# Broadcasting a gain row by products with ones, and multiplying two weight tiles on half the tokens before the other half is normed

## The chip, the cores and the metric

The kernel runs on one core of one Trainium2 chip. The metric is the device time of one execution in microseconds (us). A core has these engines, by the names of the profile: PE (TensorE, matrix products; its weight loads are listed apart as PEld), DVE (VectorE), ACT (ScalarE), POOL (GpSimd) and SP (SyncE, which here issues the DMAs). Each engine works through its own queue of instructions in a fixed order, and waits at an instruction whose semaphores have not come.

## The reference, cut to what matters

The program is one layer of a hybrid encoder on 1024 tokens of width 1024 in fp32: a mixer of windowed attention and a bidirectional gated DeltaNet, then cross attention into 256 memory tokens, then a SwiGLU network.

```
def _rms_norm(x, gain):
    xf = x.astype(jnp.float32)
    y = xf * lax.rsqrt(jnp.mean(xf * xf, axis=-1, keepdims=True) + EPS)
    return (y * gain.astype(jnp.float32)).astype(x.dtype)
...
        h = _rms_norm(x, g_mix_pre[l])
        proj = h @ w_in[l]
        aq, ak, av, dqkv, dgate, dalpha, dbeta = jnp.split(proj, IN_SPLITS, axis=-1)
...
        mix = jnp.concatenate([attn_o, dn_o], axis=-1) @ w_out[l]
        x = x + _rms_norm(mix, g_mix_post[l])
```

The change touches the first two lines of the layer: the input norm, and the first two 128-column tiles of `dqkv` (the first key head and the first query head), which a convolution over five tokens follows.

## The kernel before, in words

Every fp32 operand of a product is split into a high part, rounded by ACT, and a low part, the difference, made by DVE or POOL (`split`, lines 102 and 103). A product of two such operands is three PE products: high with high, low with high, high with low. The tiles are named by it: `hhi` and `hlo` hold the normed input, with tokens on the free axis, and `whi` and `wlo` a weight tile.

The order of the work is not written by hand. The program is written step by step, a scheduler with a timeline simulation puts the instructions of each engine in a static order when the program is built, and a tile pool (a number of buffers under one tag) adds the waits for a free buffer. `tc.high_priority` moves weight loads ahead in that order, and `tc.issue_after(i)` keeps the instructions inside it behind instruction i.

The start works as follows.

- SP loads x in eight tiles of 128 tokens (`xt`, 512 KB each, six buffers, lines 205 and 217), and `gmix` (line 207), the gain row copied to all 128 partitions by the DMA itself: 512 KB written for a row of 4 KB.
- For each tile t, ACT squares it and sums (line 220), POOL makes the reciprocal root `rs` in two small instructions (`rstd_of`, lines 159 and 160), and DVE multiplies the tile with `rs` and `gmix` in place (line 223, the scaling). PE transposes the tile in eight 128x128 pieces into two PSUM banks of the pool `ps` (line 228), ACT casts each bank to `hhi`, and DVE subtracts to give `hlo`.
- Two weight tiles of `w_in` are loaded (`load_w`), rounded on ACT and subtracted on DVE. Then `gemm_b` (line 260) multiplies: tile 1 and tile 0 on tokens 0 to 511, 24 products each, then both on tokens 512 to 1023. The results stay in the PSUM pool `pg` of three banks.
- `conv` (lines 275 to 287) reads each pair of accumulators with ACT (`cp` and `acc`, lines 282 and 283, one of each for each half), then DVE adds four taps (line 285).

In the program's text all eight tiles are normed first, and the products come after. In the static order PE has two products ahead of the last transposes, and the transposes of tiles 6 and 7 between products of the first half.

Between about 400 and 620 us lie the DeltaNet scan, the attention windows (scores `psw`, transposed probabilities `ptw`, outputs `pow`, copied to `ao` and stored to the DRAM tile `d_mix`) and the memory keys and values. The values are `pcv` (line 907); ACT copies them to `vv` (line 911, one buffer) and SP stores them to `d_mv` (line 912). After it the mixer's output product `pmg` (line 994) reads `d_mix` back: `mraw` (line 1033) is split into `b`, and the weights `w_out` are loaded by `load_w`.

Of the kernel before, what the change touches and what calls it, by code (L numbers as in the profile page):

```python
# [10 lines left out]
F32 = mybir.dt.float32  # L11
F32R = mybir.dt.float32r
I32 = mybir.dt.int32
AF = mybir.ActivationFunctionType
ALU = mybir.AluOpType
# [4 lines left out]
P = 128  # L20
S = 1024
D = 1024
KT = D // P
# [3 lines left out]
EPS = 1e-6  # L27
# [48 lines left out]
def tile_hybrid_block(  # L76
# [6 lines left out]
    nc = tc.nc  # L83
    x, mem, out = x[0], mem[0], out[0]
    w_in, w_out, w_cq, w_ckv, w_co = w_in[0], w_out[0], w_cq[0], w_ckv[0], w_co[0]
    w_gate_up, w_down = w_gate_up[0], w_down[0]

    if dump is None:
        def dump(name, ap):
            pass  # L90


    def f32(ap):
        return ap.bitcast(F32)
# [4 lines left out]
    def split(hi, lo, src, scale=None, eng=None):  # L99

        if scale is None:
            nc.scalar.copy(hi, src)  # L102
            (eng or nc.vector).tensor_tensor(lo, src, f32(hi), ALU.subtract)  # L103
        else:
            nc.scalar.activation(hi, src, AF.Identity, scale=scale)
            nc.vector.scalar_tensor_tensor(lo, src, scale, f32(hi), ALU.mult, ALU.subtract)

    def pool(name, bufs, **kw):
        return tc.tile_pool(name=name, bufs=bufs, reuse_waits="tile", **kw)
# [8 lines left out]
    def load_w(src, k, n, eng=None, after=None):  # L118

        with tc.high_priority(AHEAD):  # L120
            raw = wp.tile([P, k, n], F32, tag="wraw", name="wraw")
            with ExitStack() as order_:
                if after:
                    order_.enter_context(tc.issue_after(after.ins))
                nc.sync.dma_start(raw, src.rearrange("(k p) n -> p k n", p=P))
            hi = wp.tile([P, k, n], F32R, tag="whi", name="whi")
            lo = wp.tile([P, k, n], F32R, tag="wlo", name="wlo")
            split(hi, lo, raw, eng=eng)
        return hi, lo
# [26 lines left out]
    def rstd_of(rs, ss, n, eps):  # L156

        w = ss.shape[-1]
        nc.gpsimd.tensor_scalar(rs, ss, n, eps, ALU.mult, ALU.add)
        nc.gpsimd.tensor_tensor(rs, rs, mhalf[:, :w], ALU.pow)  # L160
# [30 lines left out]
    pg = pgs.enter_context(pool("pg", 3, space=PSUM))  # L191
# [3 lines left out]
    t1 = pa1.enter_context(pool("t1a", 2, side="right"))  # L195

    def small():
        return ps.tile([P, 512], F32, tag="ps", name="ps")


    xts = [t1.tile([P, D], F32, tag="xt", name="xt", bufs=6) for _ in range(6)]
    gmix = t1.tile([P, D], F32, tag="gmix", name="gmix", bufs=1)
    xload = []
    for t in range(6):
        xload.append(nc.sync.dma_start(xts[t], x[t * P:(t + 1) * P, :]))
        if t == 0:
            nc.sync.dma_start(gmix, g_mix_pre[0].partition_broadcast(P))
            nc.sync.dma_start(ident, consts[:, 0:P])
    hT = []
    for hf in range(2):  # L210
        hi = hx.tile([P, KT, HALF], F32R, name=f"hhi{hf}")
        lo = hx.tile([P, KT, HALF], F32R, name=f"hlo{hf}")
        for j in range(4):
            t = 4 * hf + j
            xt = xts[t] if t < 6 else t1.tile([P, D], F32, tag="xt", name="xt", bufs=6)
            if t >= 6:
                nc.sync.dma_start(xt, x[t * P:(t + 1) * P, :])
            junk = t1.tile([P, D], F32, tag="junk", name="junk", bufs=1)
            ss = t1.tile([P, 1], F32, tag="ss", name="ss", bufs=4)
            nc.scalar.activation(junk, xt, AF.Square, accum_out=ss)  # L220
            rs = t1.tile([P, 1], F32, tag="rs", name="rs", bufs=4)
            rstd_of(rs, ss, 1.0 / D, EPS)
            nc.vector.scalar_tensor_tensor(xt, xt, rs, gmix, ALU.mult, ALU.mult)
            for kq in range(2):
                pt = small()
                for k in range(4):
                    c = (4 * kq + k) * P
                    nc.tensor.transpose(pt[:, k * P:(k + 1) * P], xt[:, c:c + P], ident)
                o = slice(4 * kq, 4 * kq + 4), slice(j * P, (j + 1) * P)
                split(hi[:, o[0], o[1]], lo[:, o[0], o[1]], pt.rearrange("p (k t) -> p k t", k=4))  # L230
        hT.append((hi, lo))
        dump(f"hT{hf}", (hi, lo))


    rows = early.tile([P, P], F32, name="rows")
    nc.gpsimd.memset(rows, 0.0)
# [4 lines left out]
    pt = small()  # L241
# [13 lines left out]
    def gemm_b(whi, wlo, act, psums, nk=KT):  # L255

        for ah, p_ in zip(act, psums):
            for k in range(nk):
                for i, (w, a) in enumerate(((whi, 0), (whi, 1), (wlo, 0))):
                    nc.tensor.matmul(p_, w[:, k, :], ah[a][:, k, :], start=(k == 0 and i == 0),  # L260
                                     stop=(k == nk - 1 and i == 2))

    def proj(src_cols, eng=None):
# [2 lines left out]
        gemm_b(whi, wlo, hT, pp)  # L266
        return pp

    pa1.close()
    tb = p12.enter_context(pool("tb", 1))  # L270
    pp_ = ExitStack()
# [3 lines left out]
    def conv(pp, ci):  # L275
        cp = tcv.tile([P, S + 4], F32, tag="cp", name="cp", bufs=2)
        nc.gpsimd.memset(cp[:, 0:2], 0.0)
        nc.gpsimd.memset(cp[:, S + 2:S + 4], 0.0)
        acc = tcv.tile([P, S], F32, tag="acc", name="acc", bufs=3)
        taps = [cols[:, t * 12 + ci:t * 12 + ci + 1] for t in range(5)]  # L280
        for hf in range(2):
            nc.scalar.copy(cp[:, 2 + hf * HALF:2 + (hf + 1) * HALF], pp[hf])
            nc.scalar.activation(acc[:, hf * HALF:(hf + 1) * HALF], pp[hf], AF.Identity, scale=taps[2])  # L283
        for t in (0, 1, 3, 4):
            nc.vector.scalar_tensor_tensor(acc, cp[:, t:t + S], taps[t], acc, ALU.mult, ALU.add)  # L285
        nc.scalar.activation(acc, acc, AF.Silu)
        return acc

    def dcols(i, h):
        return w_in[:, 768 + (4 * i + h) * P:768 + (4 * i + h + 1) * P]  # L290


    ws = [load_w(dcols(i, 0), KT, P, after=xload[t]) for i, t in ((1, 1), (0, 3))]
    pps = [[None, None], [None, None]]
    for hf in range(2):
        for i in range(2):
            pps[i][hf] = pg.tile([P, 512], F32, tag="pg", name="pg")
            gemm_b(*ws[i], hT[hf:hf + 1], [pps[i][hf]])
    kqv0 = [conv(pps[0], 4), conv(pps[1], 0)]
    pa1 = ExitStack()  # L300
    t1 = pa1.enter_context(pool("t1b", 1, side="right"))
# [8 lines left out]
    for hf in range(2):  # L310
        pp = pg.tile([P, 512], F32, tag="pg", name="pg")
        for k in range(KT):
            for a in range(2):
                nc.tensor.matmul(pp, wabr[:, k, :], hT[hf][a][:, k, :], start=(k == 0 and a == 0),
                                 stop=(k == KT - 1 and a == 1))
        nc.scalar.copy(abT[:, hf * HALF:(hf + 1) * HALF], pp[0:32, :])
    pt = small()
# [42 lines left out]
    pt = small()  # L360
# [41 lines left out]
    pt = small()  # L402
# [195 lines left out]
    def window(n, g):  # L598
# [54 lines left out]
        for j in range(nb):  # L653
            pp = pw.tile([P, 512], F32, tag="pw", name="ptw")
            for hh in range(4):
                nc.tensor.transpose(pp[:, hh * P:(hh + 1) * P], pr[hh][:, j * P:(j + 1) * P], ident)
            ph = tw.tile([P, 512], F32R, tag="ph", name="ph")
            pl = tw.tile([P, 512], F32R, tag="pl", name="pl")
            split(ph, pl, pp)
            for i, (vv, pe_) in enumerate(((vhi, ph), (vhi, pl), (vlo, ph))):  # L660
                nc.tensor.matmul(po.rearrange("p h t -> p (h t)"), vv[:, j].rearrange("p r e -> p (r e)"), pe_,  # L661
                                 start=(j == 0 and i == 0), stop=(j == nb - 1 and i == 2))
# [19 lines left out]
    def delta_proj(h):  # L682
        kqv[h] = kqv.get(h, [])
        for i in (1, 0, 2)[len(kqv[h]):]:
            kqv[h].append(conv(proj(dcols(i, h), nc.gpsimd), 4 * i + h))
# [251 lines left out]
    pg = p3.enter_context(pool("pg3", 4, space=PSUM, side="right"))  # L937
# [190 lines left out]
    def turned_k(xn, k):  # L1128
        pt = pn.tile([P, 512], F32, tag="pn", name="ptn")
        for j in range(4):  # L1130
            nc.tensor.transpose(pt[:, j * P:(j + 1) * P], xn[j][:, k * P:(k + 1) * P], ident)
        return pt

    for k in range(KT):
        pt = turned_k(xn, k)
# [5 lines left out]
    for k in range(HK):  # L1141
        p0, p1 = turned_k(xn, k), turned_k(xn, k + HK)
        g0, g1 = gain("ffn", k), gain("ffn", k + HK)
        x12, t1, t2_, t3_ = (tr.tile([P, HALF], F32, name=f"r{i}", tag=f"r{i}") for i in range(4))
# [50 lines left out]
    pg = L0.enter_context(pool("pg4", 8, space=PSUM))  # L1195

    def bank(name):
        return pg.tile([P, 512], F32, tag="pg", name=name)
# [3 lines left out]
    ws = LA.enter_context(pool("ws", 2, side="right"))  # L1202
# [92 lines left out]
    pps = [bank("pd") for _ in range(NT)]  # L1295
# [25 lines left out]
    for t in range(NT):  # L1321
# [20 lines left out]
        rs = tp_.tile([P, 1], F32, tag="frs", name="frs")  # L1342
# [38 lines left out]
```

## Time and profile before

| | us |
|---|---|
| three runs | 1642.16, 1633.44, 1635.32 |
| median | 1635.32 |
| the profiled execution | 1637.34 |
| its span in the profile | 1635.6 |
| PE busy | 1554.2 (95%) |
| DVE busy | 942.7 (58%) |
| ACT busy | 750.8 (46%) |
| POOL busy | 548.9 (34%) |

The span runs from the first to the last record of the profile; 1.7 us of the execution lie outside of it. Busy shares are means over stages with different limits: in the first 50 us PE is busy for 36.2, and over the whole span DVE, ACT and POOL have idle time that costs nothing. A line of the timeline gives a start and a duration, the engine, the line of the kernel, the operation, output and inputs with their shapes, and in brackets how long the engine stood before it and what it waited for. PE's matmuls are pipelined: a product whose record is 0.39 us long starts 0.23 us after the one before it.

### The profile page before, as it was taken

How to read it: one execution, taken by the hardware profiler on the slowest of the kernel's cores; microseconds unless marked ns; L12 is line 12 of the kernel's file. 1: busy time of each engine (PE TensorE's matmuls, PEld its weight loads, DVE VectorE, ACT ScalarE, POOL GpSimd, SP SyncE). 2: the span in 40 equal slices, each digit the busy share in tenths (PEclk: the TensorE clock that was granted, in tenths of full speed). 3: DMA queues.
4: the chain of work that ended last, by engine and by line, in shares of the span. 5: the costliest groups of instructions: out<-in, count | busy, mean ns of one | idle time of the engine just before them, and what ended most of it. 6: DMA issues, size and time to landing. Idle time of an engine off the chain costs nothing.

```text
span 1635.6 us, 21442 instructions
## 1 busy us (share of the span) xinstructions
PE 1554.2 (95%) x7690; PEld 1301.3 (80%) x7690; DVE 942.7 (58%) x1431; ACT 750.8 (46%) x1518; POOL 548.9 (34%) x501
## 2 busy tenths in 40 slices
PE   6999889999899978999999999999999999999997
PEld 5878778777799857788888777888888888888886
DVE  6855986966668745443346458776555553334332
ACT  6556552237768764554336565233333232444211
POOL 2467553334337400253202221343333441321100
PEclk9999999898999998999999999999999999999999
DMA  6134257574999593454223164442223223565452
GB/s 201 41 116 130 64 166 208 140 181 133 320 320 289 149 293 112 151 184 146 74 65 116 52 213 151 126 135 77 78 90 96 79 84 114 202 214 183 140 175 73
DMA packets 267815, 240.47 MB, mean 147 GB/s; under 512 B 43176, under 2 KB 216637, under 8 KB 267709
## 3 DMA queue, kind: packets, MB, share of 16 engines
q1 hardware_dynamic: 267709, 239.11, 47.2%
q8 instruction: 60, 0.98, 0.3%
q14 instruction: 46, 0.38, 0.1%
HBM read 177.69 MB, written 58.75 MB: 145 GB/s over the span
## 4 chain that ended last, share of the span: by engine, by line
PE 67%; DVE 9%; DMA 6%; issue 3%; ACT 3%; POOL 2%; SPq 1%; POOLq 0%; ACTq 0%; DVEq 0%
PE pmg L994 10%; PE pd L1335 8%; PE pd L1311 7%; PE pE L1165 7%; PE pD L1165 7%; PE pA L1165 6%; PE pcq L260 5%; PE pB L1165 3%; PE psc L763 3%; PE pcs L1074 1%; PE pg L260 1%; DVE acc L285 1%; PE pco L1100 1%; PE pow L661 1%; DVE tmpb L510 1%
## 5 line engine op out<-in xcount | busy, mean ns | idle before, releaser
L102 ACT CAST whi<-wraw 128x1024 fp32r<-128x1024 f32 x108 | 113.4, 1050 | 167.3 <-issue 60.0
L103 POOL TENSOR_TENSOR wlo<-wraw,whi 128x1024 fp32r<-128x1024 f32 x48 | 118.3, 2464 | 174.4 <-ACT whi L102 156.1
L260 PE MATMUL pg<-hhi,whi 128*128 128x512 f32 x352 | 141.7, 404 | 0.2 <-ACT hhi L102 0.2
L260 PE MATMUL pg<-hlo,whi 128*128 128x512 f32 x352 | 141.5, 402 | 0.0
L260 PE MATMUL pg<-hhi,wlo 128*128 128x512 f32 x352 | 141.4, 402 | 0.0
L994 PE MATMUL pmg<-whi,b 128*128 128x512 f32 x384 | 119.8, 402 | 15.2 <-ACT b L102 12.6
L103 DVE TENSOR_TENSOR wlo<-wraw,whi 128x1024 fp32r<-128x1024 f32 x60 | 74.6, 1245 | 92.6 <-ACT whi L102 88.4
L1165 PE MATMUL pA<-b,whi 128*128 128x512 f32 x352 | 109.5, 392 | 1.4 <-ACT m L1182 1.4
L994 PEld LDWEIGHTS pmg<-whi,b 128*128 128x128 f32 x384 | 73.4, 193 | 32.1 <-ACT b L102 13.4
L285 DVE SCALAR_TENSOR_TENSOR acc<-cp,cols,acc 128x1024 f32<-128x1024 f32 x48 | 75.6, 1576 | 34.3 <-ACT acc L283 33.6
L1242 POOL TENSOR_TENSOR act<-act,up 128x512 f32<-128x512 f32 x33 | 48.4, 1468 | 106.6 <-issue 57.0
L260 PEld LDWEIGHTS pg<-hhi,wlo 128*128 128x128 f32 x352 | 68.0, 193 | 13.6
L260 PEld LDWEIGHTS pg<-hhi,whi 128*128 128x128 f32 x352 | 67.8, 193 | 13.5 <-ACT hhi L102 0.4
L260 PEld LDWEIGHTS pg<-hlo,whi 128*128 128x128 f32 x352 | 67.9, 193 | 13.3
L1165 PEld LDWEIGHTS pA<-b,whi 128*128 128x128 f32 x352 | 65.3, 188 | 15.1 <-ACT m L1182 2.0
L994 PE MATMUL pmg<-wlo,b 128*128 128x512 f32 x192 | 71.3, 392 | 0.0
L1165 PE MATMUL pA<-b,wlo 128*128 128x512 f32 x176 | 68.7, 391 | 1.1 <-DVE wlo L103 1.1
L1335 PE MATMUL pd<-wdh,ath 128*128 128x512 f32 x176 | 69.4, 395 | 0.0
L1335 PE MATMUL pd<-wdh,atl 128*128 128x512 f32 x176 | 69.4, 395 | 0.0
L1335 PE MATMUL pd<-wdl,ath 128*128 128x512 f32 x176 | 69.4, 395 | 0.0
L1311 PE MATMUL pd<-dl,whi 128*128 128x512 f32 x176 | 68.5, 389 | 0.0
L1311 PE MATMUL pd<-dh,wlo 128*128 128x512 f32 x176 | 68.3, 389 | 0.0
(392 smaller groups left out, 4145.0 us busy)
## 6 DMA issues: line engine op xcount, KB each, us to landing
wraw<-in_w_gate_up_dram SPq DMA_DIRECT2D x52, 512.0 KB, 3.9
kv<-d_kv SPq DMA_DIRECT2D x32, 512.0 KB, 7.1
wraw<-in_w_in_dram SPq DMA_DIRECT2D x22, 512.0 KB, 4.2
araw<-d_act SPq DMA_DIRECT2D x22, 512.0 KB, 3.4
draw<-in_w_down_dram SPq DMA_DIRECT2D x22, 512.0 KB, 4.3
atr<-d_act SPq DMA_DIRECT2D x16, 704.0 KB, 4.8
d_act<-act SPq DMA_DIRECT2D x40, 256.0 KB, 2.3
d_kv<-kv SPq DMA_DIRECT2D x8, 1024.0 KB, 6.4
```

The costliest lines, as they stand in the source:

```text
L102: nc.scalar.copy(hi, src)
L103: (eng or nc.vector).tensor_tensor(lo, src, f32(hi), ALU.subtract)
L260: nc.tensor.matmul(p_, w[:, k, :], ah[a][:, k, :], start=(k == 0 and i == 0), stop=(k == nk - 1 and i == 2))
L285: nc.vector.scalar_tensor_tensor(acc, cp[:, t:t + S], taps[t], acc, ALU.mult, ALU.add)
L510: nc.vector.tensor_tensor(tv, A[:, j + 1:, j:j + 1].to_broadcast([P, n, j]), A[:, j:j + 1, 0:j].to_broadcast([P, n, j]), ALU.mult)
L661: nc.tensor.matmul(po.rearrange("p h t -> p (h t)"), vv[:, j].rearrange("p r e -> p (r e)"), pe_, start=(j == 0 and i == 0), stop=(j == nb ...
L763: nc.tensor.matmul(out[:, d, h, :], lt[:, d, h, :], rt[:, d, h, :], start=True, stop=True)
L994: nc.tensor.matmul(pp[t], act[a][:, k, tt], w_[:, kk, :], start=(k == 0 and i == 0), stop=(k == KT - 1 and i == 2))
L1165: nc.tensor.matmul(out_, w[a][:, k, :], xx[b_][:, k, :], start=(start and k == 0 and i == 0), stop=(k == HK - 1 and i == 2), skip_group_ch ...
L1242: nc.gpsimd.tensor_tensor(o_, o_, up, ALU.mult)
L1311: nc.tensor.matmul(pps[t], a[:, tt], b_, start=(f == 0 and i == 0), stop=(f == NF - 1 and i == 2))
L1335: nc.tensor.matmul(pp, a[:, f - f0], b_[:, f], start=(f == 0 and i == 0), stop=(f == NF - 1 and i == 2))
```

## The change

It has three parts.

1. The 512 KB load of `gmix` is replaced by a load of the row alone (`grow`, 1x1024, 4 KB). POOL fills a row of ones (`one`, 1x128), PE makes two products of one row each (ones by 512 gains) into `ps` banks, and ACT copies the banks to `gmix`.
2. The norm becomes `norm_half(hf)`. The loads of the two weight tiles and their products move up in the text: norm of tiles 0 to 3, both weight tiles on tokens 0 to 511, norm of tiles 4 to 7, both weight tiles on tokens 512 to 1023. An order is added: the square, the root and the scaling of tile t stay behind the last `hlo` of tile t-2 (tiles 4 and 5: of tile 3), so that tiles keep their order.
3. The subtraction that gives `wlo` of the second weight tile (column tile 0) goes from DVE to POOL.

```diff
@@ in split @@
-            (eng or nc.vector).tensor_tensor(lo, src, f32(hi), ALU.subtract)
+            return (eng or nc.vector).tensor_tensor(lo, src, f32(hi), ALU.subtract)
@@ the input norm @@
     gmix = t1.tile([P, D], F32, tag="gmix", name="gmix", bufs=1)
+    grow = t1.tile([1, D], F32, tag="grow", name="grow", bufs=1)
+    one = t1.tile([1, P], F32, tag="one", name="one", bufs=1)
+    nc.gpsimd.memset(one, 1.0)
...
         if t == 0:
-            nc.sync.dma_start(gmix, g_mix_pre[0].partition_broadcast(P))
+            nc.sync.dma_start(grow, g_mix_pre)
             nc.sync.dma_start(ident, consts[:, 0:P])
+
+    for c in range(0, D, 512):
+        pt = small()
+        nc.tensor.matmul(pt, one, grow[:, c:c + 512], start=True, stop=True)
+        nc.scalar.copy(gmix[:, c:c + 512], pt)
     hT = []
-    for hf in range(2):
+
+    done = []
+
+    def norm_half(hf):
...
-            nc.scalar.activation(junk, xt, AF.Square, accum_out=ss)
             rs = t1.tile([P, 1], F32, tag="rs", name="rs", bufs=4)
-            rstd_of(rs, ss, 1.0 / D, EPS)
-            nc.vector.scalar_tensor_tensor(xt, xt, rs, gmix, ALU.mult, ALU.mult)
+
+            wait = done[3] if t in (4, 5) else done[t - 2] if t > 1 else None
+            with ExitStack() as order_:
+                if wait:
+                    order_.enter_context(tc.issue_after(wait.ins))
+                nc.scalar.activation(junk, xt, AF.Square, accum_out=ss)
+                rstd_of(rs, ss, 1.0 / D, EPS)
+                nc.vector.scalar_tensor_tensor(xt, xt, rs, gmix, ALU.mult, ALU.mult)
...
-                split(hi[:, o[0], o[1]], lo[:, o[0], o[1]], pt.rearrange("p (k t) -> p k t", k=4))
+                lo_at = split(hi[:, o[0], o[1]], lo[:, o[0], o[1]], pt.rearrange("p (k t) -> p k t", k=4))
+            done.append(lo_at)
...
+    norm_half(0)
...
@@ ahead of the convolutions @@
+    ws = [load_w(dcols(i, 0), KT, P, e, after=xload[t]) for i, t, e in ((1, 1, None), (0, 3, nc.gpsimd))]
+    pps = [[None, None], [None, None]]
+    for hf in range(2):
+        if hf:
+            norm_half(1)
+        for i in range(2):
+            pps[i][hf] = pg.tile([P, 512], F32, tag="pg", name="pg")
+            gemm_b(*ws[i], hT[hf:hf + 1], [pps[i][hf]])
...
-    ws = [load_w(dcols(i, 0), KT, P, after=xload[t]) for i, t in ((1, 1), (0, 3))]
-    pps = [[None, None], [None, None]]
-    for hf in range(2):
-        for i in range(2):
-            pps[i][hf] = pg.tile([P, 512], F32, tag="pg", name="pg")
-            gemm_b(*ws[i], hT[hf:hf + 1], [pps[i][hf]])
```

In all, PE gets two instructions more, ACT two copies more, DVE has one subtraction less and POOL one more (and the memset); SP issues as many DMAs as before. As the scheduler orders the whole program again, the static orders differ in other places too. In the new order of PE stand: the two 1-row products, the transposes of tiles 0 to 3, one transpose of small parameter rows, the 48 products on tokens 0 to 511, the 32 transposes of tiles 4 to 7, the 48 products on tokens 512 to 1023. On ACT the four copies `cp` and `acc` of the first half's accumulators stand ahead of the `hhi` casts of tiles 4 to 7. Between the scan's beginning (about 400 us) and `pmg` the same instructions stand in another order on PE and SP: near its end the last `pow` come ahead of the last 20 `pcv`, and SP has the three late `mraw` loads ahead of the last two loads of `w_out` and the last two stores to `d_mv`. From `pmg` on the orders are the same.

## The prediction

> **What bounds the kernel now.** I read the busy shares first (PE 95%), then PE's busy time stretch by stretch, since only a stretch in which PE stands can give or lose time.
>
> ```profile
> 0.00:50.00 50.00, 36.21 (x173) 29.75 (x174) 35.88 (x49) 29.59 (x50) 13.73 (x34) 1.00 0.57 175
> 50.00:100.00 50.00, 47.36 (x234) 38.26 (x232) 34.01 (x42) 30.60 (x77) 27.52 (x29) 1.00 0.12 33
> 400.00:420.00 20.00, 14.96 (x71) 11.76 (x70) 9.59 (x26) 15.40 (x37) 6.46 (x9) 0.84 0.73 233
> 420.00:580.00 160.00, 153.35 (x1148) 143.73 (x1147) 120.09 (x318) 119.60 (x329) 78.18 (x84) 1.00 0.88 268
> 580.00:600.00 20.00, 17.09 (x83) 13.74 (x82) 9.76 (x20) 14.55 (x33) 0.93 (x2) 0.91 0.96 343
> 600.00:620.00 20.00, 7.64 (x30) 5.58 (x28) 9.53 (x8) 13.71 (x17) 0.00 (x0) 0.73 0.82 259
> ```
>
> Each line is one stretch: its length, then the busy time of PE, PEld, DVE, ACT and POOL, the granted clock, the DMA share and GB/s. PE loses 13.8 us in the first 50 and 26.9 us between 400 and 620 (5.0, 6.6, 2.9 and 12.4); the 1016 us behind that lose 18.1 together. So the change acts at the start, and wherever it reorders work up to 620. The timeline (start, duration, engine, line, and the idle time in front of it) shows the start:
>
> ```profile
> 6.99 1.28 DVE L223 SCALAR_TENSOR_TENSOR xt<-xt,rs,gmix 128x1024 f32<-128x1024 f32 x1 [6.99 <-POOL rs L160]
> 8.33 1.97 PE L228 MATMUL ps<-ident,xt 128*128 128x128 f32 x8 [8.33 <-DVE xt L223]
> 24.04 0.48 PE L260 MATMUL pg<-hlo,whi 128*128 128x512 f32 x1
> 30.27 1.04 PE L228 MATMUL ps<-ident,xt 128*128 128x128 f32 x8
> ```
>
> Until 24.04 PE only transposes. From there the 96 products of the first two weight tiles run without a hole, the last transposes (30.27) between them, and the next product (L314) starts at 47.36. The other hole is in the chain of waits, a start and a length on each line:
>
> ```profile
> 605.54 4.35 DMA d_mv<-vv
> 609.97 0.59 ACT vv L911
> 610.58 0.33 SPq L912
> 611.01 0.37 SPq L1033
> 611.44 6.86 DMA mraw<-d_mix
> 620.59 4.52 PE pmg L994 x14
> ```
>
> SP's queue holds the loads of `mraw` behind the last store of `d_mv`, whose data wait for a buffer; PE stands from 605.7 to 618.1.
>
> **Start, the gain row.** The 512 KB load of `gmix` goes, and what is queued behind it on SP lands sooner: `gmix` landed at 6.44 and x1, next in size, at 8.2, so by 1.5 to 1.75. But DVE's first scaling used it at 6.99, while in the changed order ACT has Square x0, Square x1, copy 1, the rounding of weight tile 1, copy 2, and DVE puts `wlo` of that tile first. Square x1 6.6 to 7.7 (1.06), copy 1, rounding 8.3 to 9.3 (1.05), copy 2 0.59 to 9.9, `wlo` (1.22) to 10.7: the first scaling starts at about 10.8, 3.8 later. The two 1-row products are of a kind that no row shows; by the pitch of the fp32 products of L763 (0.112 for 128 columns, two records each) they take 0.45 to 0.9 each, and end near 6, ahead of copy 1: nothing by either end. The `one` memset is POOL's, idle then.
>
> **Start, half 0.** DVE then has to issue four scalings (5.1), seven of the `hlo` (4.6 at 0.66), and three small ones (0.5); with about 1 for the ping-pong with ACT and PE (0.5 to 2 by the waits of 0.5 to 2.2 in that stretch) the products of half 0 run from 22.0. The ACT instruction `nega` waits for its DMA (landing 18 to 21), and the `hhi` casts of x2 and x3 are queued behind it: up to 1.2 more. So 21 to 24, against 24.04. They are 48 at 0.2265 (94 and the transposes fill 24.04 to 47.36): 10.9, to E = 32.9.
>
> **Start, half 1.** Here the change adds a wait. ACT's queue has the four copies of the two accumulators, the last of which waits for the last product of half 0, and behind it all `hhi` casts of tokens 512 to 1023. So, after E: copies 0.59 + 0.69 = 1.3, `hhi` of x4 0.5 (E+1.8), two `hlo` (E+3.1), scaling x6 1.28 (E+4.4), two `hlo` of x5 (E+5.7), scaling x7 (E+7.0), two `hlo` of x6 (E+8.3), then `hlo` of x7, for which the transposes (0.5 for a bank) and `hhi` (0.55) are done beside it: E+8.6 to 8.9. PE's 32 transposes (4.2) lie inside. In the old order this chain lay under products: 47.36 minus 24.04 has no hole. Half 1 then runs 41.6 to 52.4, so L314 starts 5 later (3 to 7). POOL and DVE are no cover for it: the convolution's first `acc` on DVE, at 46.08 now, waits for the same accumulators and comes about 5.7 later, and the PE holes at 90 to 100 (2.6) are waits for that chain, so they move along. I carry +5.
>
> **The moved `wlo`.** DVE loses 1.22, POOL gains 2.46, done by about 16 (16 products of half 0 come first): nothing by itself. Against it stands this row, a DVE instruction of 0.43 otherwise that ran beside a POOL `wlo`:
>
> ```profile
> 43.48 2.67 DVE L387 TENSOR_SCALAR rn<-ang 128x512 f32<-128x512 f32 x1
> ```
>
> So 0 to +2.2 on the DVE chain; I take 0, since the scaling-like STT (`acc`, 46.08) took its usual 1.27 next to it, and keep the rest for the range. The Trainium skill (GPSIMD Engine Reference, table entry on SBUF interfaces) says that GpSimd shares them with VectorE and contends with instructions in a 2-port mode or with two SBUF inputs. By that, the scalings of x1 or x2 would be hit and the sum would be 2.2 higher.
>
> **The clock in the gap.** The first products after the 12.4 us hole ran slow:
>
> ```profile
> 618.10 2.08 PE L994 MATMUL pmg<-whi,b 128*128 128x512 f32 x4 [12.36 <-ACT b L102]
> ```
>
> 0.52 each where later ones take 0.23, with a granted clock of 0.66 for 618 to 625; after a stand of 2.7 us (220 to 230) it stayed 1.00. In the new gap transposes come every 2 us or so, so I count 0, and up to 2.3 (nine slow products times 0.25) for the range. The Trainium skill (TensorE: Matmul & The Clock Gate, Part 1) halves the clock after an idle window of about 3.4 us and restores it after as long a busy one. By that, nothing is added while the transposes are no further apart; the two rows here agree with it.
>
> **400 to 620.** No instruction is added there, but the static orders of PE (970 instructions) and SP (190) are shuffled. At its end PE's last 20 `pcv` now come behind the last `pow`, and SP issues the three `mraw` loads ahead of the last two `w_out` and `d_mv`. So the last `ao` store does not wait for these 20 (4.5 us): 607.76 becomes 603.3, `mraw` can issue at 604.5 to 607 against 611.01, ACT's five `b` casts (4.83) end at 610 to 612, while PE still has `pcv` to do. `pmg` flows from about 612.3 to 614 where it did from 620.59: a gain of 6.5. At most it is 8.5, the hole of 12.4 less some 4 for the casts that `pmg` needs in any order. At least it is 0, since DMA is busy 0.82 to 0.96 there and the loads may land as late as before. In the middle (400 to 600) 14.5 of idle time is at stake: at best some 5 comes back (the hole at 400 to 420), at worst a wait of the 2.3 to 3.3 kind (`pow` for `ph`, `ps` for `kv`) comes in several places, +10. I take +2, one such wait. The swaps before 130 are ±1.
>
> **Sum.** The profiled execution, 1637.3 (span 1635.6 and 1.7 outside): +5.0 -6.5 +2.0 = 1637.8, that is +0.5. It lies 2.0 above the median of the runs, 1635.3. I predict 1636 in runs. 0.5% (8.2 us, about what a measurement of this kernel can tell from no change) is 1627.1 below and 1643.5 above.
>
> **Rivals.** *New holes between 400 and 620* (0.30), the slower side: ACT is busy 0.75 of that stretch and DMA 0.88, so a PE instruction put ahead of its input finds no slack. It decides when PE's idle time there, 26.9 before, grows instead of shrinking by 4.5: from 30 on, with the start's 5, the time is over 1643.5; with +5 to +10 it is 1645 to 1650. Against it: 153.35 of 160 busy, PE has much independent work there.
> *All of the tail and some of the middle comes back* (0.18): -8.5 -4, and the start loses only 3 as the holes at 90 to 130 take it up: -9.5, 1626 (1621 to 1628). For it: PE's holes at 90 to 130 are 4.3. Against: they hang on the delayed chain.
> *The early multiplication does not happen* (0.04): the chain to x3 gains nothing from the removed load and half 0 starts at 24 or later, 2.2 more by the POOL contention, 2.3 by the clock: 1639 to 1642.
>
> **Numbers.** My forecast has 0.48 (1630 to 1643). Faster: nearly all of the second rival, 0.17. Slower: most of the first and the forecast's edge, 0.29. Same: 0.54. The range 1624 to 1649 leaves out the outer ends of the two outer rivals, some 0.1 each; the likeliest case by itself has 1630 to 1643.
>
> **What would show it.** First scaling at 10.8; half-0 products dense from 22; a PE gap of 8 to 9 with transposes only, from 33; L314 at 52; the wait `pmg` for `b` down from 12.4 to some 4 or less; PE idle in 400 to 620 near 22. Wrong if half 1 follows without a gap (`hhi` of x4 not behind the copies), or if that idle time is over 30.

## The result, and the profile after

The changed kernel takes 1649.46 us (median of five runs, 1647.74 to 1655.47), against 1635.32 before. The ratio is 1.0085, with a 95% interval of 1.0066 to 1.0104: slower by 0.85%, 14 us. The profiled execution took 1648.32, with a span of 1646.6 against 1635.6, so the two traces differ by 11 us. Percentages below are of about 1637 us, so that 0.1% is 1.6 us.

The stretches of the changed kernel, with the columns of the prediction's first table (PE's busy time is the first figure behind the length):

```profile
0.00:50.00 50.00, 34.62 (x146) 27.24 (x147) 25.89 (x37) 25.31 (x44) 13.48 (x34) 0.97 0.49 153
400.00:420.00 20.00, 16.90 (x75) 13.86 (x75) 9.18 (x27) 16.02 (x42) 5.31 (x8) 0.76 0.42 116
420.00:580.00 160.00, 149.33 (x1106) 139.25 (x1105) 118.80 (x313) 115.13 (x320) 77.16 (x83) 0.96 0.85 267
600.00:620.00 20.00, 18.45 (x86) 13.79 (x85) 9.48 (x20) 12.45 (x30) 0.93 (x2) 1.00 0.65 211
620.00:640.00 20.00, 10.02 (x38) 7.82 (x37) 13.82 (x11) 13.62 (x14) 0.00 (x0) 0.74 0.70 235
```

In the first 50 us PE is busy for only 1.6 less, but it shows 27 instructions less (146 against 173): 3.75 us went into the new 1-row products, and part of the transposes ran more slowly. The hole that stood at 600 to 620 now stands at 620 to 640. Stretches of fixed time compare work that has moved, so the work was cut at the same instructions in both kernels instead:

| from, to | before, us | after, us | difference |
|---|---|---|---|
| start to the first product behind the two weight tiles (`wabr`, L314) | 47.4 | 54.4 | +7.0 |
| to the first transposes of the keys (`kv`, L464) | 47.3 | 54.3 | +7.0 |
| to the scan's first product (L763) | 320.6 | 313.7 | -6.9 |
| to the scan's last product of state and keys | 140.6 | 142.1 | +1.5 |
| to PE's last product ahead of the hole | 49.9 | 56.9 | +7.0 |
| the hole ahead of `pmg` | 12.4 | 10.0 | -2.4 |
| `pmg` to the end | 1017.5 | 1015.2 | -2.3 |

Part of the second +7.0 and of the -6.9 is work that changed its place. In the new order 17 of PE's instructions that stood behind the first transposes of the keys stand ahead of them (246 instructions in the one stretch and 1479 in the other, against 229 and 1496). With the old start and this order (the second experiment) the same two stretches take 50.8 and 314.3, so 3.5 us of the +7.0 and most of the -6.9 are the order's.

The start in the timeline of the changed kernel:

```profile
10.81 2.48 DVE L239 SCALAR_TENSOR_TENSOR xt<-xt,rs,gmix 128x1024 f32<-128x1024 f32 x2
15.81 2.20 DVE L239 SCALAR_TENSOR_TENSOR xt<-xt,rs,gmix 128x1024 f32<-128x1024 f32 x1
34.77 0.69 ACT L313 ACTIVATE acc<-pg,cols 128x512 f32<-128x512 f32 x1
35.36 2.06 ACT L102 CAST hhi<-ps 128x512 fp32r<-128x512 f32 x4
40.99 1.94 PE L244 MATMUL ps<-ident,xt 128*128 128x128 f32 x8 [1.32 <-DVE xt L239]
42.76 1.22 PE L278 MATMUL pg<-hhi,whi 128*128 128x512 f32 x2
42.96 0.38 SPq L324 DMA_DIRECT2D wab<-in_w_in_dram  x1
43.44 4.50 SPq L402 DMA_DIRECT2D posi<-in_positions_dram  x2
```

The first scaling stands at 10.81, the products of the first half run densely from 23.62 to 34.1, the casts `hhi` of tile 4 start behind the last copy `acc`, and the second half starts at 42.76. The prediction leaves out the last two lines, SP's loads of `wab` (the weights of `wabr`) and of the positions. Before, they were these:

```profile
20.97 3.19 SPq L304 DMA_DIRECT2D wab<-in_w_in_dram  x1
30.87 5.79 SPq L382 DMA_DIRECT2D posi<-in_positions_dram  x2
```

Both tiles belong to a pool that is opened after the x tiles' pool is closed, so that they can take over its memory. In the kernel before, the positions are issued 0.07 us after the end of the last scaling (29.52 and 1.28), and `wab` has long been issued. In the changed kernel `wab` waits for the end of the last transposes (40.99 and 1.94), and the positions stand behind it in SP's queue. `wab` is late in every run with the new gain row (33.07 with part 1 alone), and in none without it (21.67 with parts 2 and 3 alone). So it comes with part 1. That the two small tiles which it adds to the first pool, `grow` and `one`, shift what lies where is the likely reason, but it is not shown.

What that does behind it, on DVE and ACT of the changed kernel:

```profile
53.96 5.18 POOL L103 TENSOR_TENSOR wlo<-wraw,whi 128x1024 fp32r<-128x1024 f32 x2 [25.48 <-ACT whi L102]
54.25 2.63 DVE L405 TENSOR_SCALAR ang<-ang,CE 128x512 f32<-128x512 f32 x1
56.92 2.51 DVE L407 TENSOR_SCALAR rn<-ang 128x512 f32<-128x512 f32 x1
59.34 1.27 DVE L315 SCALAR_TENSOR_TENSOR acc<-cp,cols,acc 128x1024 f32<-128x1024 f32 x1
67.02 1.28 ACT L316 ACT_TABLE_LOAD   x1 [8.12 <-DVE acc L315]
69.27 0.56 ACT L336 COPY abT<-pg 32x512 f32<-32x512 f32 x1
```

The rotary work (`ang`, `rn`) stands ahead of the convolution's taps in DVE's queue. The first tap comes at 59.34, 13.3 later than the 46.08 of before, and ACT's copy `abT`, for which PE waits, stands behind the Silu of the tapped rows: its second piece moves from 58.22 to 69.27.

The end of the stretch in the chain of waits (start, length):

```profile
620.51 2.14 ACT b L102 x3
622.65 0.70 issue
623.35 1.99 ACT b L102 x2
625.36 0.59 ACT vv L931
625.97 4.71 DMA d_mv<-vv
630.78 0.59 ACT vv L931
631.42 8.61 PE pmg L1014 x30
```

SP's store no longer holds up `mraw`. PE now waits for the last copy `vv`, which stands in ACT's queue behind five casts `b`, the other copy, a rounding and three casts more, and then waits for its buffer (for 1.0 us).

### The profile page after: what moved, and what is told of

The parts are those of the page before. It is cut to its first block, busy times and chain, and to the rows that moved or that the text cites. A ratio compares the mean times of both kernels' runs of the same rounds, so it can differ in the third digit from the quotient of the medians.

```text
span 1646.6 us, 21443 instructions
## 1 busy us (share of the span) xinstructions
PE 1561.8 (95%) x7694; PEld 1303.2 (79%) x7694; DVE 947.8 (58%) x1430; ACT 749.9 (46%) x1520; POOL 549.1 (33%) x503
## 4 chain that ended last, share of the span: by engine, by line
PE 64%; DVE 9%; DMA 6%; ACT 3%; issue 3%; POOL 3%; SPq 1%; POOLq 0%; ACTq 0%; DVEq 0%
PE pmg L1014 9%; PE pd L1355 7%; PE pd L1331 7%; PE pE L1185 7%; PE pD L1185 7%; PE pA L1185 6%; PE pcq L278 5%; PE pB L1185 3%; PE psc L783 3%; PE pcs L1094 1%; DVE tmpb L530 1%; DVE A L532 1%; DVE acc L315 1%; PE pow L681 1%; PE pco L1120 1%
## 5 line engine op out<-in xcount | busy, mean ns | idle before, releaser
L103 DVE TENSOR_TENSOR wlo<-wraw,whi 128x1024 fp32r<-128x1024 f32 x59 | 73.3, 1245 | 99.0 <-ACT whi L102 94.7
L1014 PE MATMUL pmg<-whi,b 128*128 128x512 f32 x384 | 117.7, 396 | 12.4 <-ACT vv L931 10.0
L1014 PEld LDWEIGHTS pmg<-whi,b 128*128 128x128 f32 x384 | 72.2, 190 | 28.2 <-ACT vv L931 10.4
```

Source lines behind the costliest of these rows:

```text
L103: return (eng or nc.vector).tensor_tensor(lo, src, f32(hi), ALU.subtract)
L1014: nc.tensor.matmul(pp[t], act[a][:, k, tt], w_[:, kk, :], start=(k == 0 and i == 0), stop=(k == KT - 1 and i == 2))
```

## The experiments

In the experiments all instructions from the first convolution on could be held in one order, so that a change at the start did not shuffle the work at 400 to 620. For this, the order of each engine was read from one of the two kernels as built (`ORDER_PINNED`, a table of instructions), and set in another by issue-order edges between neighbours on an engine, which wait for nothing:

```diff
+def _keep_order(nc, tc):
...
+    for k in table:
...
+        ins = traced[len(traced) - 1 - k]
+        if last is not None:
+            tc.add_manual_dep(ins, last.name,
+                              mybir.DependencyInfo(mybir.DependencyClass.NoSync, mybir.DependencyReason.DATA))
+        last = ins
...
         tile_hybrid_block(tc, *args)
+        _keep_order(nc, tc)
```

Below, "before's order" and "the new order" mean that. Every ratio is to the kernel before on the same chip in the same minutes, with its 95% interval; places in a trace are of one profiled execution.

### Start and order apart

The first is the changed kernel with before's order from the first convolution on.

> The changed kernel, but with the issue order of every engine pinned to that of the kernel before from the first convolution on; only the start is new. Theory A (start and order add up): the first product behind the two weight tiles (wabr) stays at about 54.4 against 47.4, the wait of pmg for b is back at about 12.4, and the time is 5 to 7 us over the kernel before, 1640 to 1643. Theory B (the order alone): the 7 us of the start are taken up by later waits, the time is that of the kernel before, 1635. Theory C (the start alone): all 14 us, 1649.

Measured: 1646.77 us, ratio 1.0057 (1.0035 to 1.0079): 9 us. `wabr` stood at 54.9, the first transposes of the keys at 106.6 against 94.7, and the hole ahead of `pmg` was back at 12.7.

The second is the kernel before with the new order from there on.

> The kernel before, but with the issue order of every engine pinned to that of the changed kernel from the first convolution on; only the start is old. Theory A: wabr at 47.4, PE waits for the memory values' copy as in the changed kernel (about 10 us), the time is 4 to 9 us over the kernel before, 1639 to 1644. Theory B: 1649. Theory C: 1635.

Measured: 1640.24, ratio 1.0019 (1.0006 to 1.0033): 3 us, with a hole of 10.4. The two add up to 0.76%, inside the interval of the whole change. So theory A, in which both parts count, fits best, but neither part has the size that it gave: the start costs more than 5 to 7, and the order less than 4 to 9.

### The parts of the start

All four have before's order behind the start. Part 1 alone (gain row by products):

> The kernel before with part 1 of the change alone (gain row by two products and two copies); from the first convolution on every engine has the order of the kernel before. Theory D (the start's loss has three parts: the first scaling waits for the gain row; PE's gap between the halves; the loads of wab and positions wait for the last transpose, and the convolution's taps for the rotary chain behind them): the first scaling at 10.8 as in the changed kernel, wabr at 49 to 51, no gap, the time 2 to 4 us over the kernel before. Rival (the gap is all of it): wabr within 1 us of 47.4, no change of the time.

Measured: 1640.98, ratio 1.0013 (0.9998 to 1.0028). `wabr` at 49.4, no gap. The size fits theory D, but the interval reaches no change.

Parts 2 and 3, with the gain row by DMA as before:

> The changed kernel with its gain row broadcast by the DMA again (parts 2 and 3 alone), pinned behind as before. Theory D: first scaling at 7.0, a gap of 8 to 9 between the halves, wabr at 51 to 53, positions loaded at about 40 against 30.9, the time 5 to 8 us over the kernel before. Rival (the gain row is all of it): 47 to 48 and no change.

Measured: 1646.41, ratio 1.0049 (1.0032 to 1.0067), 8 us, `wabr` at 55.6, positions at 41.30. So the gap costs more of the start's 9 us than the gain row, and removing the gain row's part saved nothing that can be told (1.0049 against 1.0057). The first scaling was back at 6.66, but the last products of the first half still ended at 34.5, and `wabr` came 3 to 5 us later than theory D had it: the scaling of tile 3, which ran beside POOL's subtraction, took 2.98 us, and the first products of that half were slow (0.63 each until 25.5, where later ones took 0.39).

Part 3 undone:

```diff
-    ws = [load_w(dcols(i, 0), KT, P, e, after=xload[t]) for i, t, e in ((1, 1, None), (0, 3, nc.gpsimd))]
+    ws = [load_w(dcols(i, 0), KT, P, e, after=xload[t]) for i, t, e in ((1, 1, None), (0, 3, None))]
```

> The changed kernel with part 3 undone (the low part of the second weight tile on DVE), pinned behind as before, so it is to be compared with start_new_rest_old. If the POOL subtraction costs nothing, as the prediction took it: the same within 1 us (wabr 55, 1646). If it slows DVE's scalings beside it: 2 us less. If DVE is the bound: 1 us more.

Measured: 1655.93, ratio 1.0121 (1.0101 to 1.0141), slower than with part 3 by some 10 us, which none of the three cases expected. The trace shows a difference that is not the subtraction: the start's order on ACT was chosen anew, and there the square of tile 6, which waits for its load, stood ahead of both casts of tile 3 (one, in the changed kernel).

```profile
23.42 1.06 ACT L489 ACTIVATE junk<-xt 128x1024 f32<-128x1024 f32 x1 [3.00 <-DMA xt<-in_x_dram]
24.48 1.05 ACT L354 CAST hhi<-ps 128x512 fp32r<-128x512 f32 x2
```

`wabr` came at 59.4. So this run says little on POOL, and much on one place in a queue.

Then the gap itself: in the changed kernel the transposes of tiles 4 to 7 were put between the 48 products of the first half (behind 14, 19, 36 and 46 of them), and their `hhi` casts ahead of the copies of the accumulators that they had stood behind.

> The changed kernel's instructions, pinned behind as before, but in the start the transposes of tiles 4 to 7 stand between the 48 products of the first half, and the casts of those tiles ahead of the accumulators' copies. Theory D: the gap closes to 2 us, wabr at 50 to 51, positions loaded at about 38, the time 2 to 4 us over the kernel before, so 5 to 7 less than start_new_rest_old. Rival (the gain row is all of it): no better than start_new_rest_old.

Measured: 1645.05, ratio 1.0048 (1.0032 to 1.0064). The gap closed, `wabr` came at 49.5, only 2.1 late, and yet the time is 8 us over the kernel before. Theory D misses the time. The rival has the time (no better than all three parts), but not by its reason, since the gain row alone cost 2 us. PE's own delay at `wabr`, 2.1 us, is not all that is carried. Two waits of PE behind `wabr` in this run:

```profile
PE ps L597 <- ACT abT L594: 2.9, 1, 2.9
PE ps L742 <- DVE kv L735: 2.4, 2, 1.3
```

Of the waits behind `wabr`, the one for `abT` is the one that the kernel before does not have. The positions are loaded at 38.42 here, 7.5 late, and the keys' first transposes come 6.3 late.

### What carries the delay

The rotary work (two loads, 20 DVE and 4 ACT instructions) was moved behind, to 79 to 149 us on DVE in the run with the old start. This was done on the new start, on the old one, and on the one with the norm inside the half, always with before's order behind them.

> start_new_rest_old with one edit: the rotary tables (two loads of positions, 20 DVE and 4 ACT instructions) stand later on SP, DVE and ACT, among the work of 75 to 120 us; nothing else moves. Theory E (what the start's loss becomes is carried by the chain last transpose, load of positions, rotary on DVE and ACT, convolution taps behind them): the first tap comes at about 51 against 59.7, the wait of PE for abT (3.0) goes, the first transposes of keys (kv) at 100 to 102 against 106.6, the time 3 to 6 us below start_new_rest_old, 1641 to 1643. Theory F (PE's own delay of 7.5 at wabr is what is carried): kv and the time as before, 1646, within 1.5 us.

> The kernel before with the same rotary edit. Theory E: in the kernel before, too, the taps stand behind the rotary chain, but only 2 to 5 us; the time falls by 0 to 3 us, or rises by as much if the moved instructions delay what stands behind them at 80 to 115. Theory F: no change, 1636 to 1638.

> norm_inside_first_half with the same rotary edit. There wabr was at 49.5 (2 over the kernel before) and yet the time 7.9 over it, with positions loaded 7.5 later. Theory E: the time is now 1 to 3 us over the kernel before, 1639 to 1641. Theory F cannot explain 7.9 from 2; if it stays at 7 to 8, the carrier is another chain of the start (the four copies of the accumulators, or the later x7).

Measured: 1651.63, ratio 1.0082 (1.0062 to 1.0102); 1644.04, ratio 1.0035 (1.0021 to 1.0049); 1649.53, ratio 1.0074 (1.0053 to 1.0095). From `wabr` to the keys' first transposes it is 47.4, 47.5 and 47.5 us, as in the kernel before (47.3), where the new start had 51.7 and the norm inside the half 51.5. So the wait of some 4 us is made by the rotary chain ahead of the taps; that part of theory E is shown. But no time was won, and all three times lie above what theory E had. The move alone costs 0.35% on the old start, where the keys' transposes come in time (94.9) and the scan begins at 418.7 instead of 415.3. Less these 0.35%, the two new starts would be at 0.47% and 0.39%, against 0.57% and 0.48% without the move, which the intervals do not tell apart. So that the wait of 4 us costs time is not shown. With two buffers for `vv` in addition:

> The kernel before with the rotary edit and two buffers for vv, a candidate that leaves the change out. The two gains add up if they are independent: 2 us from the buffers and 0 to 3 from the rotary tables, 1633 to 1636, below both kernels.

Measured: 1642.31, ratio 1.0022 (1.0008 to 1.0037). The two edits add up, but to a loss.

So the load of the positions was made early instead, with buffers of its own for `posi`, `ang` and `rn`:

```diff
-        posi = t1.tile([P, HALF], I32, tag="posi", name="posi", bufs=1)
+        posi = early.tile([P, HALF], I32, tag="posi", name="posi", bufs=1)
```

> start_new_rest_old with the rotary work of the first half of the tokens early: positions, ang and rn have buffers of their own (not the freed ones of the x tiles), the load stands right behind the small parameter loads, and the eight DVE instructions in the stretch of 8 us in which DVE stands (28 to 36). Theory E: PE's wait for abT (3.0) goes and from wabr to the first transposes of keys it is 47 to 48 as in the kernel before (51.7 in start_new_rest_old); wabr itself stays at 55; the time is 3 to 5 us below start_new_rest_old, 1641 to 1643. Theory F (the delay at wabr is all that is carried): 1646.

> norm_inside_first_half (transposes of tiles 4 to 7 between the products of the first half) with the early load of positions in buffers of their own; the eight DVE instructions directly behind the last hlo. Theory E: wabr at 49 to 50, first transposes of keys at 97 (101.0 without), the time 2 to 4 us over the kernel before, 1639 to 1641. If the time stays at 7 to 8 over it, the carrier is not the rotary chain.

Measured: 1649.99, ratio 1.0082 (1.0065 to 1.0100), and 1641.87, ratio 1.0046 (1.0028 to 1.0065). In both, PE's wait for `abT` fell to 0.6:

```profile
PE ps L597 <- ACT abT L594: 0.6, 1, 0.6
```

But in the first the table load and the two sines on ACT now delayed the second half's casts, and `wabr` came at 58.0. In the second it came at 51.2, 1.7 later than without the edit. No time was won in either. All starts with before's order behind them, but for those with the late rotary work, which itself stands behind the keys' transposes; sorted by these:

| start | `wabr` | first `kv` | ratio |
|---|---|---|---|
| before | 47.4 | 94.7 | 1 |
| part 1 alone | 49.4 | 96.7 | 1.0013 |
| norm inside the half, rotary early | 51.2 | 100.0 | 1.0046 |
| norm inside the half | 49.5 | 101.0 | 1.0048 |
| parts 2 and 3 | 55.6 | 104.6 | 1.0049 |
| all three parts | 54.9 | 106.6 | 1.0057 |
| the same, rotary early | 58.0 | 106.8 | 1.0082 |
| part 3 undone | 59.4 | 110.2 | 1.0121 |

The time goes with the column of `kv` rather than with `wabr`. The clearest pair is part 1 alone and the norm inside the half: `wabr` is the same (49.4 and 49.5), and the intervals of the two ratios do not overlap. But `kv` does not give the size: 101.0 and 104.6 have the same ratio. Neighbouring rows can't be told apart, and the places vary too: in three traces of the changed kernel with its own order `wabr` stood at 54.4, 56.1 and 56.1. What happens between `kv` and the scan, where part of a delay is lost and part is not, stays open: two traces of the old start with one order (the kernel before, and with two buffers for `vv`) differ there by 3.2 us already (320.6 and 317.4).

### The hole ahead of `pmg`

Two buffers for `vv` (shared with the small copies of the keys, `cv`), each kernel in its own order:

```diff
-        cv = mk.tile([P, ML], F32, tag="cv", name="cv", bufs=2)
+        cv = mk.tile([P, 512], F32, tag="vv", name="cv", bufs=2)[:, 0:ML]
...
-            vv = mk.tile([P, 512], F32, tag="vv", name="vv", bufs=1)
+            vv = mk.tile([P, 512], F32, tag="vv", name="vv", bufs=2)
```

> The kernel before in its own order on every engine, but the memory values' copy vv has two buffers (shared with the small copies of the keys) in place of one, so that the last copy waits for no store. If SP's queue behind that store held up the mraw loads, as the prediction read the chain: mraw issues 2 us sooner, the hole of 12.4 shrinks by 2 to 3 us, the time by as much, 1633. If mraw waits for the last store of ao, or its transfer is slowed by DMA traffic: no change.

> The changed kernel in its own order on every engine, with two buffers for vv. If the last copy vv, 4.7 us behind a store of d_mv, is what pmg waits for (it frees the PSUM bank), the hole of 10 us shrinks by 4 to 5, the time to 1644 or 1645. If pmg then waits for something that comes as late (b, or DVE's part of it): less than 2 us, 1648 or more.

Measured: before 1635.19, ratio 0.9989 (0.9976 to 1.0002), its hole 11.0 for 12.4; the changed kernel 1653.58, ratio 1.0088 (1.0063 to 1.0113), its hole 8.8 for 10.0. So a buffer was little of it, as the second case of the second expectation has it. In the trace of the second the copy still stood behind five casts `b`, a rounding and three casts more. The copies were therefore moved ahead of the last of them on ACT, first on the old start with the new order:

> start_old_rest_new with two buffers for vv, and with the two copies vv ahead of the last three b casts on ACT (behind the first two), and the low parts of the first half's b first on DVE. If the hole ahead of pmg is these copies' place in ACT's queue (they free the PSUM banks that pmg takes), it falls from 10.4 to 3 to 6 us and the time from 1640 to 1634 to 1636, so below the kernel before. If it is the way of the last ao through DRAM (store, load mraw, cast): the hole stays at 8 or more and the time at 1638 or more.

Measured: 1647.44, ratio 1.0068 (1.0053 to 1.0082), a loss. The edit had also put the rounding of the next weight tile behind the casts:

```profile
PE pmg L1246 <- ACT b L354: 6.4, 1, 6.4
PE pmg L1246 <- ACT whi L354: 5.1, 1, 5.1
```

The hole fell to 6.4, and `pmg` began at 618.7 instead of 620.0. But from there to the end it took 1026.6 us instead of 1016.1. Of these 10.5, 5.1 are the wait for `whi`, and the eight products behind it took 3.78 where they took 1.98 without the wait:

```profile
638.51 3.78 PE L1246 MATMUL pmg<-whi,b 128*128 128x512 f32 x8 [5.13 <-ACT whi L354]
```

With the rounding back in its place only the copies move:

> old_start_new_order_copies_first with the rounding of the second w_out tile back in its place on ACT (ahead of the last three b casts), where the kernel before it had PE wait 5.1 for it; so against start_old_rest_new only the two copies vv (with two buffers) move. If the copies' place is what the hole of 10.4 is made of: a hole of 6 to 7 (the last ao through DRAM is next), no wait for whi, time 3 to 4 us below start_old_rest_new, 1636 to 1637, about the kernel before. If the wait for the weights comes back, or the hole is still 9 or more: 1640.

> The changed kernel itself with the same edit (two buffers for vv, and the two copies vv ahead of the last three b casts on ACT), nothing else moved. The hole ahead of pmg falls from 10.0 to 5 to 7, the time by 3 to 5 us, 1645 to 1647. By the rival (DRAM way of the last ao alone): no change, 1649.

Measured: 1638.28, ratio 1.0006 (0.9991 to 1.0021), hole 5.9 for 10.4; and the changed kernel 1648.04, ratio 1.0072 (1.0049 to 1.0094), hole 5.5 for 10.0:

```profile
628.98 0.80 PE L1266 MATMUL pmg<-whi,b 128*128 128x512 f32 x1 [5.53 <-ACT b L354]
```

Both holes fell by 4.5, as expected if the copies' place in ACT's queue makes them. What is left (5.5) is the way of the last `ao` through DRAM: the cast `b` that ends it waited for the load `mraw`. Of the 4.5, each median gave back more than half: the ratios fell by 0.13%, 2 us, which the intervals do not tell from 0. In the traces it is lost behind the start of `pmg`, from which it takes 1020.1 to the end instead of 1016.1, and 1016.9 instead of 1015.2. The new order with this edit is no better than the kernel before. No version was clearly faster than the kernel before; its own order with two buffers for `vv` comes closest (0.9989).

## Why the prediction was wrong

I predicted 1636 with a range of 1624 to 1649; it is 1649.46. The sum was +5.0 for the start, -6.5 for the tail and +2.0 for the middle. The runs show +9 for the start (0.57%) and +3 for the order behind it (0.19%), where I had -4.5.

**The first scaling, the first half.** Forecast 10.8 and 22.0, with 10.9 to E = 32.9; measured 10.81, 22.62 (dense from 23.62) and 34.1. The working held, though the two 1-row products took 3.75 together, not 0.9 to 1.8. Much of that is the pace of PE at the start and not the one row: the first sixteen transposes took 3.67, where eight later ones took 1.06. They were still ready ahead of the copies, which came at 8.09 and 9.54.

**The second half.** E+8.6 to 8.9 was forecast, and the first products came at E+8.7, with the casts behind the copies as described. With a slow first pair `wabr` was at 54.4, 7.0 late, the end of my range of 3 to 7.

**What the start's delay becomes: the step that failed first.** I wrote that the convolution's first `acc` would come "about 5.7 later", from the accumulators alone. It came 13.3 later. The tap stands on DVE behind the rotary work, that behind the load of the positions, and that on SP behind the load of `wab`, which waits for the last transposes. On ACT the copies of these accumulators stand behind a sine of the rotary work, too, which waited until 51.69. Even before, the tap at 46.08 did not wait for the accumulators, whose copy had ended at 44.47, but for `rn` ahead of it on DVE. The prediction does not follow SP's queue as far as `wab` and `posi`. PE then got a new wait of 1.8 to 3.0 for `abT`. In the run with before's order the delay at the keys' transposes was 12, and the time 9 us, where I carried 5. Which part of the 9 us comes by this chain stays open, since the experiments that took the wait away won no time.

**The moved `wlo`.** I took 0 and kept 2.2 for the range, since an `acc` "next to it" had taken its usual 1.27. That was misread: POOL's subtraction ran from 43.48 to 45.88, and the `acc` began at 46.08, after it. In the changed kernel the scaling of tile 2 took 2.20 beside the moved subtraction, and `ang` and `rn` 2.63 and 2.51 beside the next two, where `rn` took 0.43 by itself. The Trainium skill (GPSIMD Engine Reference, table entry on SBUF interfaces) names instructions with two SBUF inputs and those in a 2-port mode. The traces show 0.9 to 2.2 us more for a DVE instruction beside a POOL subtraction; in which mode it ran, no run shows. With part 3 undone the scaling of tile 2 took 1.27, but stood behind DVE's own `wlo` of 1.23, and ended at 18.03, against 18.26 with part 3 (both runs with before's order behind the start). So up to there part 3 made 0.2 us, and 0 was about right for the sum. What part 3 costs in the whole time was not isolated: undoing it brought another order with it, which cost more.

**The clock in the gap.** I took 0, at most 2.3, since the granted clock "stayed 1.00" after a stand of 2.7 us. That was misread: the stretch of 220 to 230 ends just behind this stand. The timeline of before goes on like this:

```profile
229.60 0.50 PE L442 MATMUL ps<-gm,mU_r 128*128 128x512 f32 x1 [2.69 <-POOL gm L441]
230.51 0.63 PE L260 MATMUL pg<-hhi,wlo 128*128 128x512 f32 x1
```

From 231 to 233 the granted clock was 0.50, and products took 0.63 instead of 0.39. The same came in the new gap, where the granted clock was 0.50 from 41 to 44. Eight transposes of tile 7 took 1.94 and the first two products 1.22, where the transposes of tiles 4 to 7 took 1.03 to 1.06 when they stood between products (norm inside the half). So the gap cost something over 1 us in this way. The Trainium skill (TensorE: Matmul & The Clock Gate, Part 1) has the clock halved after an idle window of about 3.4 us; here PE had stood for 2.6 and 1.3 only, with eight transposes between, and for 2.7 in the kernel before. In both places the traces show the halved clock, but no stand of 3.4 us in front of it.

**The tail: the second step that failed.** The term of 6.5 measured 2.4. `mraw` was issued ahead of the last `d_mv`, as I read from the order, and the casts `b` followed. But PE's `pmg` needs PSUM banks that the copies `vv` leave, and the prediction leaves out what stands ahead of these copies on ACT: eight casts and a rounding ahead of the last one. Moving the copies brought the hole nearer to the one that I had in mind (5.5 and 5.9, forecast "some 4 or less").

**The middle.** I took +2, one wait more. From the scan's last product to the hole it is 56.9 instead of 49.9. Only about 1.8 of this is idle time (6.8 against 5.1); PE's busy time rose from 44.8 to 50.1 for the same products (230 and 232 records), in groups whose mean durations rose, as here:

```profile
L661 PE MATMUL pow<-ph,vhi 128*128 128x512 f32 x11 | 4.7, 427 | 3.7 <-ACT ph L102 3.7
...
L681 PE MATMUL pow<-ph,vhi 128*128 128x512 f32 x11 | 5.8, 527 | 2.4 <-ACT ph L102 2.4
```

The upper line is of before, the lower of after (busy, mean ns, idle time). The granted clock of this stretch was 0.91 against 0.97. With the old start and the new order it is the same (55.6 us, 0.91), so the order makes it, and not the start.

**The rivals.** The slower side came, with 0.29 on it. My rival for it, new holes of 3 us or more in PE's idle time between 400 and 620, is not how: between the scan's first product and `pmg` PE stood 23.6 instead of 21.9, and the order's cost was slower products and a tail that closed only in part. The early multiplication did happen, and the rival in which everything came back did not.

## What to carry to other kernels

When work is moved past a point, look for what reuses its memory: a load that takes over buffers moves with their last reader, and with it what stands behind that load in its queue. When a wait is expected to close, list what the waiting instruction needs in all (operands, weights, and the banks that it writes), and what stands ahead of each of these in its engine's queue. And where a scheduler orders the whole program again, hold the old order behind the change before judging the change: here 3 of the 12 us that the two halves add up to were an order that nobody had asked for.

## What the runs showed of the hardware

Two fp32 products with one row each (1x128 by 1x512) took 3.75 us together in four records, 0.94 a record, at the very start, where the reading from later products gave half of that at most. Transposes there also took about twice their later time (0.23 each against 0.13), though the granted clock is shown as 1.00 for this stretch. After a stand of 2.69 us, and after stands of 2.60 and 1.32 with eight transposes between, the granted clock fell to 0.50. DVE instructions of 128x512 that take 0.42 to 0.49 us by themselves took 2.5 to 2.7 beside a POOL subtraction of 128x1024, once in the kernel before and twice in the changed one. And a stretch of PE in which short stops alternate with work lost 5.3 us in longer products and 1.8 in stops, so the waits alone would have told a quarter of it.
